# First-layer attention: VectorE in program order, low parts at fixed places, one step for the products with v

## The chip, the cores and the metric

One core of one Trainium2 chip runs the whole kernel. The metric is the device time of one execution in microseconds (us), median of several. In this text PE is the matmul engine (TensorE), DVE is VectorE, ACT is ScalarE, POOL is GpSimd, SP is the engine that issues the loads.

## The reference

Four sandwich-normed layers over x of 1 x 256 x 1024, float32. Each layer does `h = h + rms_norm(mixer(rms_norm(h)))`; the mixer differs by layer. The change touches the first, native sparse attention, with 16 heads of 64 in 4 groups that share keys and values:

```python
q, kc, vc, ks, vs, kw, vw, gl, z = split_cols(u @ w_in, A_SPLITS)
kcmp, vcmp = compress(kc, ...), compress(vc, ...)      # 15 blocks of 32 tokens, gelu MLP
p_c = masked_softmax(q @ kcmp - slopes * dist, dist >= 0);  o_c = p_c @ vcmp
p_s = masked_softmax(q @ ksel - slopes * dist, dist >= 0);  o_s = p_s @ vsel
p_w = masked_softmax(q @ kwin - slopes * dist, mask);       o_w = p_w @ vwin
o = gates[0] * o_c + gates[1] * o_s + gates[2] * o_w   # gates = sigmoid(gl)
return (o * silu(z)) @ w_out
```

At 256 tokens the selected blocks and the window each cover all earlier tokens, so both are plain causal softmaxes with their own keys and values.

## The kernel before, in words

**Products in two parts.** A weight tile of 128 x 1024 is loaded into a `raw` buffer (5 of them), ACT writes its rounded high part `whi`, DVE the rest `wlo` (line 106, "low part" from here on); there are 11 pairs of buffers. A projection then does three matmuls per 128 rows (`mm3`, lines 200 to 202: one *step*). `advance()` (line 68) runs at the end of each weight tile: it gives up the tile's pair of buffers, splits the next tile into parts and issues the next load. A load waits until the low part of the tile five places ahead of it has left its `raw` buffer. Tiles are numbered here by their place in the load list: 26 to 31 are the q projections of groups 1 to 3, 32 to 39 the projections for z, 40 to 47 the weights of the output projection, 48 on the next layer's.

**The stage.** After the compression of the keys and values, the pairs of heads 0 to 7 (`nsa_unit`; pair p belongs to group p // 2) run as a pipeline. The front of a pair is three pieces: `scores_of(0, (0, 1))` (queries 0 to 127, both heads), `scores_of(1, (0,))` and then `finish` (queries 128 to 255, one head each; `finish` also scales all the weights by gate over sum, lines 797 to 807). Each makes one score tile in PSUM per head, `S`, of which there are two buffers; per tile DVE adds the mask and takes the minimum twice (line 294), then ACT the exponentials (line 296). An even pair has `cmp_front` ahead of these (the 15 compressed keys: score, two bias steps, softmax on DVE). The back of a pair is two pieces with transposes (`trans`, line 301) and two with the products with v (`pv`, lines 317, 320; the second adds the compressed branch, line 819); an even pair has `cmp_back` ahead of these.

**Order.** `pipeline` lays the pieces of pair i's front (F) and of pair i-1's back (B) out by the pattern `FFBFBBB` and puts steps of the waiting projections between them from a queue (`fill`, `pop`): two after each piece at first, later one. PE's instructions are issued in exactly the order in which the program is written. On ACT, DVE and POOL the scheduler picks, by readiness in its own model and by priority; low parts and high parts of weights have the priority `LATE = -250`, what the z gate needs `LATEZ = -60`, copies out of PSUM `EARLY = 80`.

**Other places that the change touches.** `keep_q` (line 639) takes a q projection out of PSUM: ACT makes the scaled high part, DVE the low part (line 644). `Gate` multiplies attention output and silu(z) (`silu_tanh`, line 392; line 351) and splits the result into parts for the output projection (lines 359, 360).

Of the kernel before, what the change touches and what calls it, by code (L numbers as in the profile page):

```python
# [10 lines left out]
F32 = mybir.dt.float32  # L11
# [17 lines left out]
POOLED = (6,)  # L29
# [8 lines left out]
def trunk(ctx, tc, I, out):  # L38
# [23 lines left out]
    for n in "bcd":  # L62
        add(n + "_v", *range(8))
        add(n + "_t", *range(20 if n == "c" else 24))
        add(n + "_o", *range(8))
    st = {"load": 0, "split": 0, "next": 0, "held": 0, "parts": 0, "after": [], "most": len(seq)}
    raw, parts = {}, {}

    def advance(most=len(seq)):
        while True:  # L70
            while st["load"] < min(len(seq), st["split"] + NS - st["held"] + max(0, min(3, 8 - st["split"]))):
                i = st["load"]
                if i == X1AT:
                    nc.sync.dma_start(h[:, 1, :], I["x"][1])
                _, k, c = seq[i][0].shape
                if 5 <= i < 8:
                    if i == 5:
                        st["extra"] = big.tile([128, 3, 560], F32, name="oT")
                    t = st["extra"][:, i - 5, :]
                else:  # L80
                    t = wts.tile([128, 1024], F32, name="raw", bufs=NS)[:, :k * c]
                t = t.rearrange("p (k c) -> p k c", k=k)
                dma = nc.sync.dma_start(t, seq[i][0])
                if i == 7:
                    st["dma"] = dma.ins
                raw[i] = t
                st["load"] += 1
            i = st["split"]
            if i >= st["load"] or st["parts"] >= NH or i >= min(most, st["most"]):
                return  # L90
            t = raw.pop(i)
            st["split"] += 1
            if not seq[i][1]:
                parts[i] = t
                st["held"] += 1
                continue
            _, k, c = seq[i][0].shape
            hi, lo = [wts.tile([128, 1024], F32R, name=n, bufs=NH)[:, :k * c].rearrange("p (k c) -> p k c", k=k)
                      for n in ("whi", "wlo")]
            with ExitStack() as after:  # L100
                after.enter_context(tc.high_priority(offset=LATE if i >= 12 else 0))
                for ins in st["after"]:
                    after.enter_context(tc.issue_after(ins))
                ACT.activation(hi, t, AF.Copy)  # L104
                on_pool = i in POOLED
                lo_of = (POOL if on_pool else DVE).tensor_tensor(lo, t, hi.bitcast(F32), op=OP.subtract)  # L106
                if i == max(POOLED):
                    st["pool"] = lo_of.ins
                elif not on_pool:
                    st["lo"] = lo_of.ins  # L110
            parts[i] = (hi, lo)
            st["parts"] += 1

# [101 lines left out]
    def pop():  # L215
        fq.popleft()()
        plan["count"] += 1

    def drain():
        while fq:  # L220
            pop()

    def need(i):

# [3 lines left out]
    def push_proj(use, q=fq, idx=None):  # L228

        t = {}  # L230
        idx = idx or take(2)

        def step(c, k):
            if c == 0 and k == 0:
                t["o"] = ps.tile([128, 2, 256], F32, name="mm", bufs=NMM)
            wh, wl = parts[idx[c]]
            mm3(t["o"][:, c, :], wh[:, k, :], wl[:, k, :], uT[0][:, k, :], uT[1][:, k, :], k == 0, k == 7)
            if k == 7:
                free(idx[c])
                if c == 1:  # L240
                    use(t["o"])
                advance()

        for c in range(2):
            for k in range(8):
                q.append(lambda c=c, k=k: step(c, k))
# [76 lines left out]
    class Gate:  # L323
# [9 lines left out]
                push_proj(lambda z, i=i: self.have_z(i, z))  # L333

        def have_z(self, i, z):
            with tc.high_priority(offset=LATEZ):
                self.w[i] = self.silu(z)
            self.go()

        def have_o(self, p):  # L340
            self.o.add(p)
# [14 lines left out]
        def split(self, i):  # L356
            g, hi, lo = [t[:, 2 * i:2 * i + 2, :] for t in (self.oT, *self.gh)]
            with tc.high_priority(offset=LATEZ):
                ACT.activation(hi, g, AF.Copy)
                DVE.tensor_tensor(lo, g, hi.bitcast(F32), op=OP.subtract)  # L360

        def open(self):

# [25 lines left out]

    tanhs = []  # L390

    def silu_tanh(z):
        w = work.tile([128, 2, 256], F32, name="zw", bufs=2)
        tanhs.append(ACT.activation(w, z, AF.Tanh, scale=0.5))
        DVE.scalar_tensor_tensor(w, w, 1.0, z, op0=OP.add, op1=OP.mult)
        return w

    def out_proj(g, l):
        last = l == 3
# [161 lines left out]
    for hd in range(16):  # L561
        POOL.memset(slc[:, hd // 4, hd % 4:hd % 4 + 1], SLA[4 * (hd // 4) + hd % 2])
    dcmp = const.tile([128, 2, 2, 15], F32, name="dcmp")
    d0 = dcmp[:, 0]
    POOL.iota(d0, pattern=[[-128, 2], [16, 15]], base=31, channel_multiplier=-1,
              allow_small_or_imprecise_dtypes=True)
    POOL.affine_select(out=d0, in_=d0, pattern=[[128, 2], [-16, 15]], base=-31, channel_multiplier=1,
                       fill=NEG, compare_op=OP.is_ge)
    POOL.tensor_scalar(dcmp[:, 1], d0, 0.5, None, op0=OP.mult)
    bm = const.tile([60, 4], F32, name="bm")  # L570
    POOL.memset(bm, 0.5)
    POOL.affine_select(out=bm, in_=bm, pattern=[[-15, 4]], base=0, channel_multiplier=1, fill=0.0,
# [63 lines left out]
    def keep_q(o, g):  # L636


        for j in range(2):
            r, other = HALF[j], HALF[1 - j]  # L640
            hs = slice(4 * g + j, 4 * g + j + 3, 2)
            hi, sc = t["q"][r, hs, :], cq[r, 2 * g:2 * g + 1]
            ACT.activation(hi, o[r], AF.Copy, scale=sc)
            DVE.scalar_tensor_tensor(t["q"][other, hs, :], o[r], sc, hi.bitcast(F32), op0=OP.mult,
                                     op1=OP.subtract)
        ready[g] = plan["count"]

    t = {}
# [65 lines left out]
            f()  # L714
    for g in range(1, 4):
        push_proj(lambda o, g=g: keep_q(o, g))
    for _ in range(9):
        pop()
    hidden_t()
# [4 lines left out]

    ga = Gate(0.5, silu_tanh)
    ga.push()
    CS, PTC = {}, {}

    def cmp_front(g):

# [7 lines left out]
        cs = CS[g] = work.tile([128, 2, 4, 15], F32, name="cs", bufs=2)  # L738
        two = sc[:, 0:256].rearrange("p (a s n) -> p a n s", s=2, n=16)[:, :, 0:15, :]
        DVE.tensor_reduce(out=cs.rearrange("p b a n -> p (b a) n"), in_=two, axis=AX.X, op=OP.add)  # L740
        for b in range(2):
            for c in range(2):
                DVE.tensor_tensor(cs[:, b, 2 * c:2 * c + 2], cs[:, b, 2 * c:2 * c + 2],
                                  dcmp[:, c, b, None, :].to_broadcast([128, 2, 15]), op=OP.add)
        for b in range(2):
            DVE.tensor_tensor(cs[:, b], cs[:, b], slc[:, g, :, None].to_broadcast([128, 4, 15]), op=OP.mult)
        cs8 = cs.rearrange("p b a n -> p (b a) n")
        cm, cl = small(8, "cm", 2), small(8, "cl", 2)
        DVE.tensor_reduce(out=cm, in_=cs8, axis=AX.X, op=OP.max)
        DVE.tensor_scalar(cm, cm, -1e20, None, op0=OP.max)  # L750
        DVE.tensor_tensor(cs8, cs8, cm[:, :, None].to_broadcast([128, 8, 15]), op=OP.subtract)
        ACT.activation(cs, cs, AF.Exp)
        DVE.tensor_reduce(out=cl, in_=cs8, axis=AX.X, op=OP.add)
        DVE.tensor_scalar(cl, cl, 1e-30, None, op0=OP.max)
        DVE.reciprocal(cl, cl)
# [11 lines left out]
    def nsa_unit(p):  # L767
# [25 lines left out]

        def finish():
            scores_of(1, (1,))
            l = t["l"]
            DVE.reciprocal(l, l)
            gv = bass.AP(tensor=gate.tensor, offset=gate.offset + 16 + 2 * p,
                         ap=[list(gate.ap[0]), [1, 2], [16, 2], [48, 2]])
            DVE.tensor_tensor(l.rearrange("p (j r b) -> p j r b", j=2, r=2),  # L800
                              l.rearrange("p (j r b) -> p j r b", j=2, r=2), gv, op=OP.mult)
            for br in range(2):
                for j in range(2):
                    x = (j * 2 + br) * 2
                    P = t["P"][j, br]
                    DVE.tensor_scalar(P[:, 0:128], P[:, 0:128], l[:, x:x + 1], None, op0=OP.mult)  # L806
                    DVE.tensor_scalar(P[:, 128:384], P[:, 128:384], l[:, x + 1:x + 2], None, op0=OP.mult)
# [4 lines left out]
        def pv(br):  # L812
            if br == 0:
                t["o"] = ps.tile([128, 256], F32, name="o", bufs=1)
            o = t["o"]
            pv_pair(o, t["PT", br], v, (br * 256 + g * 64,) * 2, br == 0, False)
            if br == 1:
                for j in range(2):
                    PE.matmul(o[64 * j:64 * j + 64, :], vbd[g][:, 2 * i + j, :], PTC[g], start=False, stop=True)
                evac(ga.oT[:, p, :], o)  # L820
                ga.have_o(p)

        front = [lambda: scores_of(0, (0, 1)), lambda: scores_of(1, (0,)), finish]
        back = [lambda: trans(0), lambda: trans(1), lambda: pv(0), lambda: pv(1)]
        if i == 0:
            front.insert(0, lambda: cmp_front(g))
            back.insert(0, lambda: cmp_back(g))
        return front, back

    trans = out_proj(pipeline([nsa_unit(p) for p in range(8)], ga, "FFBFBBB"), 0)  # L830


    SLB = slopes_of(8)
# [190 lines left out]
        with tc.issue_after(pre.ins):  # L1024
            return ACT.activation(*a, **k)

    def silu_sigmoid(z):
        w = work.tile([128, 2, 256], F32, name="zw", bufs=2)
        after_table(w, z, AF.Sigmoid)
        DVE.tensor_tensor(w, w, z, op=OP.mult)  # L1030
        return w

    v = v_proj(trans)
    kT = big.tile([128, 8, 256], F32, name="kT")
# [123 lines left out]
```

## Time and profile before

| | |
|---|---|
| median of 3 runs | 581.54 us (581.32 to 582.4) |
| the profiled execution, own time | 583.38 us |
| its span, first to last instruction | 581.7 us |
| PE busy | 560.6 us, 96% of the span, granted clock 0.992 on average |
| DVE busy | 420.3 us, 72% |
| ACT busy | 334.5 us, 58% |
| POOL busy | 40.7 us, 7% |
| the loads (queue 1) | 86.09 MB, 43.7% of the 16 DMA engines' time |

The span is the stretch that the trace covers; the execution's own time is 1.7 us longer. The share of busy time is a mean over stages. The chain that ended last is 81% PE, 8% DVE, 4% issue, 2% ACT, 2% DMA. The stage of the change begins some 62 us into the span and ends at 165.19 us, with the first matmul of the output projection.

### The profile page before, as it was taken

The numbers are of one execution on the slowest core, as the hardware profiler recorded it, in microseconds if no ns is written. First come the engines' busy times: TensorE is split into PE (matmuls) and PEld (weight loads), VectorE is DVE, ScalarE is ACT, GpSimd is POOL, SyncE is SP. The second block draws the span as 40 slices with busy tenths as digits, with TensorE's granted clock in tenths as the row PEclk, the third lists the DMA queues.
The fourth block names the chain that finished last, engine by engine and source line by source line (L and its number), as shares of the span: only waits on it lengthen the run. The fifth ranks groups of instructions, "written<-read, shape, count | busy, mean of one in ns | idle before, by whom it ended". The sixth has DMA issues, their size and how long they took to land.

```text
span 581.7 us, 10475 instructions
## 1 busy us (share of the span) xinstructions
PE 560.6 (96%) x3930; PEld 496.8 (85%) x3930; DVE 420.3 (72%) x947; ACT 334.5 (58%) x715; POOL 40.7 (7%) x89
## 2 busy tenths in 40 slices
PE   7999987989999999999999999999999999999995
PEld 6998876777788799999988789999987898888984
DVE  5973898887836896777974886768548778888632
ACT  6752787776824475676642474658524765666410
POOL 1900000000000100000420100000001000000000
PEclk9999998999999999999999999999999999999998
DMA  8774925521250596443352568443525683332002
GB/s 296 247 251 146 319 71 190 168 90 44 74 179 4 180 330 231 147 145 126 120 171 73 181 238 302 149 145 110 177 76 181 233 307 137 120 110 74 1 37 73
DMA packets 27779, 90.96 MB, mean 156 GB/s; under 512 B 4560, under 2 KB 5200, under 8 KB 27728
## 3 DMA queue, kind: packets, MB, share of 16 engines
q1 hardware_dynamic: 26144, 86.09, 43.7%
q10 hardware_dynamic: 1584, 4.20, 2.2%
q8 instruction: 31, 0.51, 0.4%
q14 instruction: 20, 0.16, 0.1%
HBM read 89.22 MB, written 1.05 MB: 155 GB/s over the span
## 4 chain that ended last, share of the span: by engine, by line
PE 81%; DVE 8%; issue 4%; ACT 2%; DMA 2%; POOL 1%; SPq 0%; POOLq 0%; DVEq 0%; ACTq 0%
PE mm L200 16%; PE mm L201 14%; PE mm L202 14%; PE mm L262 6%; PE mm L260 6%; PE mm L261 6%; PE pt L301 3%; DVE wlo L106 3%; PE S L311 3%; PE o L317 2%; ACT whi L104 1%; PE o L655 1%; DVE P L294 1%; DMA h<-in_x_dram 1%; PE pt L188 1%
## 5 line engine op out<-in xcount | busy, mean ns | idle before, releaser
L200 PE MATMUL mm<-uth,whi 128*128 128x256 f32 x736 | 219.0, 298 | 0.0
L106 DVE TENSOR_TENSOR wlo<-raw,whi 128x1024 fp32r<-128x1024 f32 (+1 forms) x153 | 182.3, 1207 | 43.4 <-ACT whi L104 42.8
L201 PE MATMUL mm<-utl,whi 128*128 128x256 f32 x736 | 208.5, 283 | 0.0
L202 PE MATMUL mm<-uth,wlo 128*128 128x256 f32 x736 | 208.3, 283 | 0.0
L104 ACT ACTIVATE whi<-raw 128x1024 fp32r<-128x1024 f32 (+1 forms) x153 | 157.0, 1043 | 73.5 <-PE mm L201 38.5
L200 PEld LDWEIGHTS mm<-uth,whi 128*128 128x128 f32 x736 | 140.9, 191 | 15.5 <-issue 14.7
L201 PEld LDWEIGHTS mm<-utl,whi 128*128 128x128 f32 x736 | 141.1, 192 | 0.9
L202 PEld LDWEIGHTS mm<-uth,wlo 128*128 128x128 f32 x736 | 140.9, 191 | 0.0
L260 PE MATMUL mm<-whi,qT 128*128 128x512 f32 x128 | 50.5, 394 | 0.0
L261 PE MATMUL mm<-whi,kT 128*128 128x512 f32 x128 | 49.9, 390 | 0.0
L262 PE MATMUL mm<-wlo,qT 128*128 128x512 f32 x128 | 49.9, 390 | 0.0
L260 PE MATMUL mm<-whi,uth 128*128 128x512 f32 (+1 forms) x112 | 42.6, 380 | 0.0
L262 PE MATMUL mm<-wlo,uth 128*128 128x512 f32 (+1 forms) x112 | 42.1, 376 | 0.0
L261 PE MATMUL mm<-whi,utl 128*128 128x512 f32 (+1 forms) x112 | 42.1, 376 | 0.0
L294 DVE CUSTOM_DVE_ANT_0 P<-S,mask 128x128 f32<-128x128 f32 (+1 forms) x96 | 30.6, 353 | 8.3 <-PE S L786 6.0
L415 ACT ACTIVATE junk<-mm 128x512 bf16<-128x512 f32 x16 | 9.5, 595 | 42.1 <-PE mm L262 42.1
L296 ACT ACTIVATE P<-P,mxa 128x128 f32<-128x128 f32 (+1 forms) x64 | 28.4, 447 | 3.7 <-DVE mxa L294 3.7
L146 ACT ACTIVATE PT<-pt 128x384 f32<-128x384 f32 x58 | 25.8, 483 | 7.5 <-PE pt L301 7.5
L262 PEld LDWEIGHTS mm<-wlo,qT 128*128 128x128 f32 x128 | 24.0, 188 | 5.0
L260 PEld LDWEIGHTS mm<-whi,qT 128*128 128x128 f32 x128 | 24.1, 188 | 4.7
L261 PEld LDWEIGHTS mm<-whi,kT 128*128 128x128 f32 x128 | 24.1, 188 | 4.7
L301 PE MATMUL pt<-ident,P 128*128 128x128 f32 x180 | 27.0, 279 | 0.5 <-DVE P L806 0.4
(207 smaller groups left out, 757.3 us busy)
## 6 DMA issues: line engine op xcount, KB each, us to landing
raw<-in_a_t_dram SPq DMA_DIRECT2D x24, 512.0 KB, 4.8
raw<-in_b_t_dram SPq DMA_DIRECT2D x24, 512.0 KB, 4.6
raw<-in_d_t_dram SPq DMA_DIRECT2D x24, 512.0 KB, 4.5
raw<-in_c_t_dram SPq DMA_DIRECT2D x20, 512.0 KB, 5.2
raw<-in_w_dram SPq DMA_DIRECT2D x8, 512.0 KB, 4.7
raw<-in_a_o_dram SPq DMA_DIRECT2D x8, 512.0 KB, 3.8
raw<-in_b_v_dram SPq DMA_DIRECT2D x8, 512.0 KB, 3.4
raw<-in_b_o_dram SPq DMA_DIRECT2D x8, 512.0 KB, 3.5
```

The lines of the kernel that those rows point to most:

```text
L104: ACT.activation(hi, t, AF.Copy)
L106: lo_of = (POOL if on_pool else DVE).tensor_tensor(lo, t, hi.bitcast(F32), op=OP.subtract)
L146: ACT.activation(dst, src, AF.Copy)
L200: PE.matmul(o, sh, mh, start=first, stop=False)
L201: PE.matmul(o, sh, ml, start=False, stop=False)
L202: PE.matmul(o, sl, mh, start=False, stop=last)
L260: PE.matmul(o, sh, wh[:, j, c0:c1], start=k == 0, stop=False)
L261: PE.matmul(o, sl, wh[:, j, c0:c1], start=False, stop=False)
L262: PE.matmul(o, sh, wl[:, j, c0:c1], start=False, stop=k == 7)
L294: DVE.tensor_tensor_reduce(out=P[:, c0:c1], in0=S, in1=mask[:, c0:c1], scale=-slope, scalar=BIG, op0=OP.add, op1=OP.min, accum_out=mx)
L296: ACT.activation(P[:, c0:c1], P[:, c0:c1], AF.Exp, bias=mx, scale=-1.0, accum_out=l)
L301: PE.transpose(pt[:, i, :], P[:, i * 128:(i + 1) * 128], ident)
```

## The change

Within the stage, DVE's instructions too are now issued in the order of the program (`manual_schedule` from the 15 steps ahead of `cmp_front(0)` to the end of the pipeline). Low parts of weights that are split within the stage are kept back and written at set places: one in `first` (unless the second half of the compressed softmax stands there), one in `second`, one in `finish` ahead of the scaling, and in any case when the tile or the one before it begins; what is left comes at the stage's end. What DVE does with a result of ACT (low part of q, silu, low part of the gated output) is written three steps later (`later(3, ...)`); the second half of the compressed softmax comes after the first scores of the pair. Six small additions and multiplications per group become two. Both products with v of a pair are one piece, and the pattern is `FFBFBB`. In the other layers the same functions run at once.

```diff
+    def low_parts(n):
+        for i in sorted(low)[:n]:
+            low.pop(i)()
+    def later(n, f):
+        if st["own"]:
+            waiting.append((plan["count"] + n, f))
+        else:
+            f()
+    def overdue(everything=False):
+        while waiting and (everything or waiting[0][0] <= plan["count"]):
+            waiting.popleft()[1]()
...
                 ACT.activation(hi, t, AF.Copy)
-                on_pool = i in POOLED
-                lo_of = (POOL if on_pool else DVE).tensor_tensor(lo, t, hi.bitcast(F32), op=OP.subtract)
...
+                low[i] = lambda i=i, t=t, hi=hi, lo=lo: low_part(i, t, hi, lo)
+                if not st["own"]:
+                    low.pop(i)()
...
     def pop():
         fq.popleft()()
         plan["count"] += 1
+        overdue()
...
+            for i, at in ((idx[c], 0), (idx[c] + 1, 2)):
+                if k == at and i in low:
+                    low.pop(i)()
             wh, wl = parts[idx[c]]
             mm3(t["o"][:, c, :], wh[:, k, :], wl[:, k, :], uT[0][:, k, :], uT[1][:, k, :], k == 0, k == 7)
...
+    own = ExitStack()
+    own.enter_context(tc.manual_schedule(engines={mybir.EngineType.DVE}))
+    st["own"] = True
     for _ in range(9):
         pop()
     hidden_t()
...
-        for b in range(2):
-            for c in range(2):
-                DVE.tensor_tensor(cs[:, b, 2 * c:2 * c + 2], cs[:, b, 2 * c:2 * c + 2],
-                                  dcmp[:, c, b, None, :].to_broadcast([128, 2, 15]), op=OP.add)
-        for b in range(2):
-            DVE.tensor_tensor(cs[:, b], cs[:, b], slc[:, g, :, None].to_broadcast([128, 4, 15]), op=OP.mult)
+        pairs = cs.rearrange("p b (c j) n -> p (b c) j n", j=2)
+        DVE.tensor_tensor(pairs, pairs, dcmp.rearrange("p b c n -> p (b c) n")[:, :, None, :]
+                          .to_broadcast([128, 4, 2, 15]), op=OP.add)
+        DVE.tensor_tensor(cs, cs, slc[:, g, None, :, None].to_broadcast([128, 2, 4, 15]), op=OP.mult)
...
         ACT.activation(cs, cs, AF.Exp)
+        CHALF.append(lambda: cmp_weights(g, cs, cs8, cl))
...
         def finish():
             scores_of(1, (1,))
+            low_parts(1)
             l = t["l"]
             DVE.reciprocal(l, l)
...
+        def pvs():
+            pv(0)
+            pv(1)
...
+        def first():
+            scores_of(0, (0, 1))
+            if CHALF:
+                CHALF.pop()()
+            else:
+                low_parts(1)
+        def second():
+            scores_of(1, (0,))
+            low_parts(1)
-        front = [lambda: scores_of(0, (0, 1)), lambda: scores_of(1, (0,)), finish]
-        back = [lambda: trans(0), lambda: trans(1), lambda: pv(0), lambda: pv(1)]
+        front = [first, second, finish]
+        back = [lambda: trans(0), lambda: trans(1), pvs]
...
-    trans = out_proj(pipeline([nsa_unit(p) for p in range(8)], ga, "FFBFBBB"), 0)
+    gh = pipeline([nsa_unit(p) for p in range(8)], ga, "FFBFBB")
+    low_parts(len(seq))
+    st["own"] = False
+    own.close()
+    trans = out_proj(gh, 0)
```

The low parts of `keep_q`, of silu and of the gated output are wrapped in `later(3, ...)` in the same way.

## Rows read from the trace of the kernel before

**Rows 1.** Part 1 of the page: engine, busy us (share of the span), instructions.
```profile
PE 560.6 (96%) x3930; PEld 496.8 (85%) x3930; DVE 420.3 (72%) x947; ACT 334.5 (58%) x715; POOL 40.7 (7%) x89
```

**Rows 2.** Windows: stretch, length, busy PE, PEld, DVE, ACT, POOL; clock, DMA share, GB/s.
```profile
62.00:102.00 40.00, 33.52 (x258) 30.26 (x258) 36.93 (x120) 32.38 (x77) 0.00 (x0) 0.96 0.53 184
102.00:162.00 60.00, 57.66 (x440) 45.56 (x441) 49.27 (x207) 43.57 (x135) 1.16 (x4) 1.00 0.31 98
```

**Rows 3.** Timeline of PE, 79 to 98 us: start, length, engine, line, [idle <-releaser].
```profile
79.31 0.40 PE L785 MATMUL S<-kT,qT 128*128 128x512 f32 x1
...
92.43 0.39 PE L785 MATMUL S<-kT,qT 128*128 128x256 f32 x1 [1.12 <-DVE cs L740]
...
97.79 0.77 PE L785 MATMUL S<-kT,qT 128*128 128x512 f32 x1 [2.78 <-DVE cm L750]
```

**Rows 4.** Windows of PE alone around 98 us: stretch, length, busy, clock, DMA, GB/s.
```profile
98.00:98.60 0.60, 0.60 (x2) 0.50 0.77 314
...
100.40:101.00 0.60, 0.60 (x7) 0.68 0.00 0
```

**Rows 5.** Timeline of DVE, 69 to 87 us.
```profile
69.83 1.40 DVE L701 TENSOR_TENSOR v<-o,bm 60x256 f32<-60x256 f32 x4
...
77.71 0.42 DVE L294 CUSTOM_DVE_ANT_0 P<-S,mask 128x256 f32<-128x256 f32 x1
...
79.34 1.18 DVE L106 TENSOR_TENSOR wlo<-raw,whi 128x1024 fp32r<-128x1024 f32 x1
...
83.03 3.50 DVE L106 TENSOR_TENSOR wlo<-raw,whi 128x1024 fp32r<-128x1024 f32 x3
```

**Rows 6.** Timeline of SP, the loads from 84 us.
```profile
84.74 2.24 SPq L83 DMA_DIRECT2D raw<-in_a_t_dram  x3
```

**Rows 7.** Timeline of ACT, the high part that waits for such a load.
```profile
89.10 1.06 ACT L104 ACTIVATE whi<-raw 128x1024 fp32r<-128x1024 f32 x1 [1.59 <-DMA raw<-in_a_t_dram]
```

**Rows 8.** Timeline of DVE, end of pair 4, its scaling, and that of pair 7.
```profile
126.49 0.42 DVE L294 CUSTOM_DVE_ANT_0 P<-S,mask 128x256 f32<-128x256 f32 x1 [1.61 <-PE S L786]
...
127.18 0.29 DVE L294 CUSTOM_DVE_ANT_0 P<-S,mask 128x128 f32<-128x128 f32 x1
...
127.39 0.29 DVE L294 CUSTOM_DVE_ANT_0 P<-S,mask 128x128 f32<-128x128 f32 x1
...
130.32 0.28 DVE L806 TENSOR_SCALAR P<-P,la 128x128 f32<-128x128 f32 x1
...
132.16 0.42 DVE L294 CUSTOM_DVE_ANT_0 P<-S,mask 128x256 f32<-128x256 f32 x1
...
154.22 0.20 DVE L797 RECIPROCAL la<-la 128x8 f32<-128x8 f32 x1
...
154.65 0.29 DVE L806 TENSOR_SCALAR P<-P,la 128x128 f32<-128x128 f32 x1
```

**Rows 9.** Timeline of PE, scores of pair 5.
```profile
127.41 0.36 PE L785 MATMUL S<-kT,qT 128*128 128x256 f32 x1 [0.37 <-DVE mxa L294]
...
128.08 0.40 PE L785 MATMUL S<-kT,qT 128*128 128x512 f32 x1
```

**Rows 10.** Groups by line and form, 62 to 162 us: busy, mean ns | idle before.
```profile
L644 DVE SCALAR_TENSOR_TENSOR qT<-mm,cq,qT 64x512 fp32r<-64x512 f32 x8 | 6.0, 750 | 0.7 <-ACT qT L643 0.5
...
L743 DVE TENSOR_TENSOR cs<-cs,dcmp 128x30 f32<-128x30 f32 x16 | 1.9, 185 | 0.0
```

**Rows 11.** Timeline of PE around the two products with v of one pair.
```profile
112.75 0.28 PE L201 MATMUL mm<-utl,whi 128*128 128x256 f32 x1
112.86 0.28 PE L202 MATMUL mm<-uth,wlo 128*128 128x256 f32 x1
...
113.56 0.39 PE L320 MATMUL o<-PT,v 128*64 128x128 f32 x4
113.87 0.39 PE L200 MATMUL mm<-uth,whi 128*128 128x256 f32 x1
...
114.42 0.65 PE L317 MATMUL o<-PT,v 128*64 128x256 f32 x4
```

More of the change, by code (lines that the diff above doesn't have):

```diff
@@ L65, in trunk, with low_part @@
         add(n + "_o", *range(8))
-    st = {"load": 0, "split": 0, "next": 0, "held": 0, "parts": 0, "after": [], "most": len(seq)}
-    raw, parts = {}, {}
+    st = {"load": 0, "split": 0, "next": 0, "held": 0, "parts": 0, "after": [], "most": len(seq), "own": False}
+    raw, parts, low = {}, {}, {}
+    waiting = deque()
+    def low_part(i, t, hi, lo):
+        on_pool = i in POOLED
+        lo_of = (POOL if on_pool else DVE).tensor_tensor(lo, t, hi.bitcast(F32), op=OP.subtract)
+        if i == max(POOLED):
+            st["pool"] = lo_of.ins
+        elif not on_pool:
+            st["lo"] = lo_of.ins
+    def low_parts(n):
[9 more added lines that the diff above has]
+            waiting.popleft()[1]()
     def advance(most=len(seq)):
@@ L104, in advance @@
                 ACT.activation(hi, t, AF.Copy)
-                on_pool = i in POOLED
-                lo_of = (POOL if on_pool else DVE).tensor_tensor(lo, t, hi.bitcast(F32), op=OP.subtract)
[L107 to L110, printed above, removed]
+                low[i] = lambda i=i, t=t, hi=hi, lo=lo: low_part(i, t, hi, lo)
+                if not st["own"]:
+                    low.pop(i)()
             parts[i] = (hi, lo)
@@ L221, in drain @@
             pop()
+        overdue(True)
     def need(i):
@@ L335, in have_z, with got @@
         def have_z(self, i, z):
+            def got(w):
+                self.w[i] = w
+                self.go()
             with tc.high_priority(offset=LATEZ):
-                self.w[i] = self.silu(z)
-            self.go()
+                self.silu(z, got)
         def have_o(self, p):
@@ L359, in split @@
                 ACT.activation(hi, g, AF.Copy)
-                DVE.tensor_tensor(lo, g, hi.bitcast(F32), op=OP.subtract)
+                later(3, lambda: DVE.tensor_tensor(lo, g, hi.bitcast(F32), op=OP.subtract))
         def open(self):
@@ L390, in trunk, with silu_tanh, rest @@
     tanhs = []
-    def silu_tanh(z):
+    def silu_tanh(z, got):
         w = work.tile([128, 2, 256], F32, name="zw", bufs=2)
         tanhs.append(ACT.activation(w, z, AF.Tanh, scale=0.5))
-        DVE.scalar_tensor_tensor(w, w, 1.0, z, op0=OP.add, op1=OP.mult)
-        return w
+        def rest():
+            DVE.scalar_tensor_tensor(w, w, 1.0, z, op0=OP.add, op1=OP.mult)
+            got(w)
+        later(3, rest)
     def out_proj(g, l):
@@ L563, in trunk @@
     dcmp = const.tile([128, 2, 2, 15], F32, name="dcmp")
-    d0 = dcmp[:, 0]
+    d0 = dcmp[:, :, 0]
     POOL.iota(d0, pattern=[[-128, 2], [16, 15]], base=31, channel_multiplier=-1,
@@ L568, in trunk @@
                        fill=NEG, compare_op=OP.is_ge)
-    POOL.tensor_scalar(dcmp[:, 1], d0, 0.5, None, op0=OP.mult)
+    POOL.tensor_scalar(dcmp[:, :, 1], d0, 0.5, None, op0=OP.mult)
     bm = const.tile([60, 4], F32, name="bm")
@@ L643, in keep_q @@
             ACT.activation(hi, o[r], AF.Copy, scale=sc)
-            DVE.scalar_tensor_tensor(t["q"][other, hs, :], o[r], sc, hi.bitcast(F32), op0=OP.mult,
-                                     op1=OP.subtract)
+            later(3, lambda r=r, other=other, hs=hs, hi=hi, sc=sc: DVE.scalar_tensor_tensor(
+                t["q"][other, hs, :], o[r], sc, hi.bitcast(F32), op0=OP.mult, op1=OP.subtract))
         ready[g] = plan["count"]
@@ L726, in trunk @@
     ga.push()
-    CS, PTC = {}, {}
+    CS, PTC, CHALF = {}, {}, []
     def cmp_front(g):
@@ L752, in cmp_front, with cmp_weights @@
         ACT.activation(cs, cs, AF.Exp)
+        CHALF.append(lambda: cmp_weights(g, cs, cs8, cl))
+    def cmp_weights(g, cs, cs8, cl):
         DVE.tensor_reduce(out=cl, in_=cs8, axis=AX.X, op=OP.add)
@@ L816, in pv @@
             pv_pair(o, t["PT", br], v, (br * 256 + g * 64,) * 2, br == 0, False)
[L817 to L821, printed above, removed]
-        front = [lambda: scores_of(0, (0, 1)), lambda: scores_of(1, (0,)), finish]
-        back = [lambda: trans(0), lambda: trans(1), lambda: pv(0), lambda: pv(1)]
+        def pvs():
+            pv(0)
+            pv(1)
+            o = t["o"]
+            for j in range(2):
+                PE.matmul(o[64 * j:64 * j + 64, :], vbd[g][:, 2 * i + j, :], PTC[g], start=False, stop=True)
+            evac(ga.oT[:, p, :], o)
+            ga.have_o(p)
+        def first():
[9 more added lines that the diff above has]
+        back = [lambda: trans(0), lambda: trans(1), pvs]
         if i == 0:
@@ L1025, in after_table, with silu_sigmoid @@
             return ACT.activation(*a, **k)
-    def silu_sigmoid(z):
+    def silu_sigmoid(z, got):
         w = work.tile([128, 2, 256], F32, name="zw", bufs=2)
@@ L1030, in silu_sigmoid @@
         DVE.tensor_tensor(w, w, z, op=OP.mult)
-        return w
+        got(w)
     v = v_proj(trans)
```

## The prediction

> **What bounds the kernel now.** I read the page first: PE is busy 96% of the span, so time is gained only where PE stands still, runs at the lower clock, or has less to do [rows 1]. Next, windows over the stage that is changed. It falls in two. From 62 to 102 us PE worked 33.52 of 40 us while DVE worked 36.93: DVE is the bound there, and PE lost 6.48 us. From 102 to 162 us PE worked 57.66 of 60 and DVE 49.27: PE is the bound and lost only 2.34 us [rows 2]. So all that better order on DVE can give back is 6.48 + 2.34 = 8.8 us, and what the clock cost. Then the timeline, for who is waited for: PE's score matmuls wait for DVE, 1.12 us at 92.43 and 2.78 us at 97.79 [rows 3]. Both are the same wait: there are two `S` buffers, and a third score tile cannot begin until DVE has taken its two minima of the first. After the second wait the granted clock is 0.50 (1.2 GHz) and comes back about 100.8 [rows 4]; 3.0 us at half speed cost about 1.45 us.
>
> **The change, part by part.** I wrote out both programs' order for the stage, piece by piece, with the queue's counts; the steps and pieces below are from there.
>
> *Products with v in one piece.* Before, the last matmuls of the first product start at 113.56, one step lies between, and the second product starts at 114.42: 0.86 us. Without the step the next thing starts 0.31 us later (113.56 to 113.87). The step that is moved costs three matmuls at a pitch of 0.11 to 0.12, 0.36 us, elsewhere [rows 11]. Saved: 0.86 - 0.31 - 0.36 = 0.19 us a pair, 1.5 us for eight pairs, all on PE. The step between hid ACT's copies of the second pair of transposes; if that cover fails, the 0.19 is lost again, so -1.5 to 0. I take **-1.5**.
>
> *The scaling now stands ahead of the next pair's minima.* This is the largest part. After an even pair's `finish` come, with one step between each (two for pair 2), the odd pair's `first` and `second`. `second`'s score tile needs the buffer that the minima of `first` free. Before, DVE took these minima as soon as the scores were there (127.18) and did low part and scaling later [rows 8]. Now the program's order holds: two minima of pair 4 (126.49 to 127.18, 0.69), a low part (a third of 3.50, 1.17, [rows 5]), reciprocal and gate until the scaling starts (154.22 to 154.65, 0.43), eight scalings (130.32 to 132.16, 1.84), two minima of pair 5 (2 x 0.21 from 127.18 to 127.39, 0.42) [rows 8]. That is 4.55 us one after another, from 126.49 to 131.04. PE had issued this score tile at 128.08 [rows 9]: it comes 3.0 us later, and nothing lies on PE to fill the time, since its order is fixed and everything behind this matmul waits too. Pair 6 to 7 has the same order: 3.0. Between pairs 2 and 3 the two low parts of q stand there as well (2 x 0.750, [rows 10]) and PE has one more step to do: 3.0 + 1.5 - 0.36 = 4.1. Together +10.1. What goes: the later half's idle time, 2.34 less the 0.37 that pairs 5 and 7 each have inside the figure above [rows 9], 1.6. So **+8.5** (7 to 10: below, if ACT or PE is late anyway; above, if DVE also waits for the exponentials ahead of the reciprocal).
>
> *Low parts at fixed places, early stretch.* Before, DVE finishes the four copies `v` at 71.2 and does no low part until 79.34; by then it has the last minima of pair 0 behind it (77.71 + 0.42 = 78.1) [rows 5], so that the `second` scores of pair 1 start at 79.31 [rows 3]. Now the low part of tile 37 must come ahead of those last minima of pair 0, and that of 38 and the scaling of pair 0 ahead of pair 1's first. Tile 37 is not there yet: its load waits for the buffer of tile 32, hence for the low parts of 31 and 32, which the scheduler still places itself. From such a load's issue (84.74, [rows 6]) to the end of its high part (89.10 + 1.06, [rows 7]) is 5.4 us. Either the low parts of 31 to 36 fill DVE's gaps ahead of it, or DVE stands and takes them then. Upper end: eight low parts (31 to 38) x 1.17 = 9.4, with 0.43 + 1.84 + 0.42 for scaling and minima, less 0.5 for the merged small instructions (next part): 78.1 + 11.6 = 89.7 against 79.31, +10.4. Lower end: five low parts (31 to 33, 37, 38), +6.9. I take the middle, +8.6. DVE has then done work that it did later before, so the waits of 1.12 and 2.78 and the 1.45 of the clock go: -5.35. Net **+3.2** (1.5 to 5.0).
>
> *Clock.* PE now stands for about 3 us or more four times (at the end of the early stretch, and at pairs 3, 5 and 7). The one such wait of before, 2.78 us, was followed by the lower clock at a cost of 1.45 [rows 3, 4]. Between nothing and 4 x 1.45 = 5.8 I take 0.85 each, **+3.4**, since the clock may be up again before the wait ends. The Trainium skill ("TensorE: Matmul & The Clock Gate", section "Part 1: The HAM clock gate") says that an idle PE is put to the lower clock and gets the higher one back only by sustained work. Rows 3 and 4 agree for their one case; by the rule all four would pay in full, and the sum would be 2.4 higher.
>
> *Merged small instructions.* Sixteen additions of 185 ns become four, eight multiplications four [rows 10]; four instructions fewer a group, up to 0.74 us of DVE less what the larger ones take longer: 0 to 0.74. I count 0.5 in group 0 (above) and nothing for groups 1 to 3, where PE has transposes and steps to do meanwhile. The Trainium skill ("Perfetto Trace Analysis", section "Optimizing Scalar/DVE Operations") holds that grouping into larger operations pays where the engine is saturated. By rows 2 that is the early stretch; by the rule group 1 would count too, and the sum would be 0.5 lower.
>
> *The rest, at 0.* Low parts of q, silu and gated output three steps later: they replace waits of DVE for ACT, and PE needs them a whole tile later; if that cover is gone one instruction of 0.75 [rows 10] is in the way each time. Low parts of 48 to 50 at the stage's end hold back three loads; the output projection hides them, and uncovered they cost one such load, 5.4 us. In layers 2 to 4 the gating runs at a lower priority than before, at most one low part (1.17) either way in each.
>
> **Sum.** -1.5 + 8.5 + 3.2 + 3.4 = +13.6 us. The profiled execution took 583.38 us in all (span 581.7 and 1.7 around it), so 597.0 for such a one. The median of the runs shown is 581.54, 1.8 below it: **595.1 us**.
>
> **Rivals.**
> (a) *Milder*: few low parts get ahead early (+1.5 net), the clock holds: 1.5 + 8.5 - 1.5 = +8.5, 590.0 us. For it: 1.12 us of waiting left no trace on the clock. Against: the new waits are longer than the 2.78 that did.
> (b) *Worse*: upper ends everywhere, 5.0 + 10 + 5.8 - 1.5 = +19.3, 600.8 us. For it: ACT's high part of 1.06 us may stand ahead of an exponential that DVE's fixed order now waits for.
> (c) *Faster*: the low parts fall into gaps ahead of 71 us and DVE no longer lets the small instructions of the compressed softmax come between two minima, so the `S` buffers come free in time. Place: the early stretch; price: all of its loss, 6.48 + 1.45 = 7.9; with 1.6 and 1.5 from above that is -11.0 against +10.1, 580.6 us. It decides as soon as pair 1's `second` scores start no later than 79.3 and the scaling costs the next pair no more than it gives back. Against it: 36.93 of 40 us leaves DVE no gap for six low parts [rows 2].
> (d) *Nothing*: the scheduler's order was in effect the program's. Against: it took the minima ahead of the scaling at 127.18 [rows 8]. 581.5 us.
>
> **How the numbers follow.** Forecast 0.42 (its own range 591 to 599), (a) 0.24, (b) 0.17, (c) 0.13, (d) 0.04. The range runs from a little below (a) to the top of (b), 584 to 603; outside lie (c), (d) and the far end of (b). About 0.2% (1.2 us) can be told from no change by a measurement of this kernel: faster 0.13, same 0.04, slower 0.83.
>
> **What would show it.** In the profile after: the `second` score tile of pairs 3, 5 and 7 preceded by 3 to 4 us of idle PE that a minimum of DVE ends, with eight scalings and a low part just ahead of that minimum; three or four stretches at a clock of 0.5; the stage's end, 165.19 before, about 13 to 14 us later, and everything behind it shifted by that. The products with v would follow each other 0.31 us after the last matmuls of the first. I am wrong if PE's idle time from 62 us to the output projection is no more than 8.8 us, or if these score tiles do not wait.

## The result and the profile after

The changed kernel took **603.38 us** (602.38 to 603.81, 4 runs) against 581.97 us for the kernel before (581.32 to 585.17, 4 runs): a ratio of 1.0354, interval 1.0313 to 1.0395. It is slower, as forecast, but by 21.4 us and not by 13.6. The profiled execution took 602.38 us, its span is 600.7 us: 19.0 more than the one before, at a mean granted clock of 0.974 (0.992 before).

Part 1 of the page of the changed kernel; it answers to [rows 1]:
```profile
PE 564.7 (94%) x3930; PEld 502.5 (84%) x3930; DVE 422.0 (70%) x931; ACT 335.0 (56%) x715; POOL 41.4 (7%) x89
```
The work is the same, PE just stands still longer. Where, the windows say (columns as in [rows 2]); the second one here runs to the stage's end, which is later than before:
```profile
62.00:102.00 40.00, 28.53 (x193) 25.34 (x193) 33.09 (x92) 26.29 (x57) 0.00 (x0) 0.79 0.57 203
102.00:185.00 83.00, 70.47 (x524) 60.05 (x525) 53.78 (x217) 51.55 (x153) 1.16 (x4) 0.92 0.17 53
```
In the early stretch PE now loses 11.47 us (6.48 before), and DVE, which bounded it, is busy *less*: 33.09 of 40 us against 36.93. So it isn't that DVE has more to do; it does it in another order, with waits of its own. Windows of PE alone over the whole stage, up to the first matmul of the output projection, first of the kernel before, then of the changed one (stretch, length, busy, clock, DMA, GB/s). On PE's timeline this matmul starts at 165.03 before; the 165.19 above is the chain's time for it:
```profile
62.00:165.03 103.03, 94.21 (x721) 0.98 0.39 129
```
```profile
62.00:184.00 122.00, 97.99 (x712) 0.87 0.30 103
```
The stage ends 18.97 us later: 15.19 us of it is idle time (24.01 against 8.82), the other 3.78 are PE's busy time, whose matmuls last longer at the lower clock. The timeline of PE in the changed kernel names the waits, which answer to [rows 3, 9]:
```profile
77.62 0.76 PE L823 MATMUL S<-kT,qT 128*128 128x512 f32 x1 [5.59 <-DVE mxa L321]
...
83.91 0.36 PE L823 MATMUL S<-kT,qT 128*128 128x256 f32 x1 [2.20 <-DVE mxa L321]
...
85.73 0.55 PE L823 MATMUL S<-kT,qT 128*128 128x256 f32 x1 [1.35 <-DVE mxa L321]
...
89.56 0.77 PE L823 MATMUL S<-kT,qT 128*128 128x512 f32 x1 [1.78 <-DVE mxa L321]
...
118.45 0.77 PE L823 MATMUL S<-kT,qT 128*128 128x512 f32 x1 [5.03 <-DVE mxa L321]
...
144.35 0.47 PE L823 MATMUL S<-kT,qT 128*128 128x512 f32 x1 [3.01 <-DVE mxa L321]
...
166.21 0.71 PE L823 MATMUL S<-kT,qT 128*128 128x512 f32 x1 [3.01 <-DVE mxa L321]
```
All are score matmuls that wait for minima (`mxa`) of DVE. The summary of PE's waits puts it in one row (total, times, longest):
```profile
PE S L823 <- DVE mxa L321: 23.2, 10, 5.6
```
What stood ahead of the minima is in the timeline of DVE. In the early stretch:
```profile
70.47 1.21 DVE L72 TENSOR_TENSOR wlo<-raw,whi 128x1024 fp32r<-128x1024 f32 x1
71.60 0.27 DVE L779 TENSOR_TENSOR cs<-cs,dcmp 128x120 f32<-128x120 f32 x1
71.79 1.21 DVE L72 TENSOR_TENSOR wlo<-raw,whi 128x1024 fp32r<-128x1024 f32 x1
...
75.65 1.21 DVE L72 TENSOR_TENSOR wlo<-raw,whi 128x1024 fp32r<-128x1024 f32 x1
...
76.98 0.27 DVE L321 CUSTOM_DVE_ANT_0 P<-S,mask 128x128 f32<-128x128 f32 x1
...
79.17 0.28 DVE L791 TENSOR_REDUCE cl<-cs 128x8 f32<-128x120 f32 x1 [1.28 <-ACT cs L787]
```
Five low parts of 1.21 us stand between the small dependent instructions of the compressed scores, which follow each other within 0.2 to 0.3 us where nothing stands between them. They are written ahead of the region with the fixed order, so they still go where the scheduler puts them; experiment 5, which holds them back, moves them out of these gaps. At pairs 3 and 5:
```profile
113.86 0.20 DVE L836 RECIPROCAL la<-la 128x8 f32<-128x8 f32 x1 [0.63 <-ACT P L323]
...
116.25 1.51 DVE L678 SCALAR_TENSOR_TENSOR qT<-mm,cq,qT 64x512 fp32r<-64x512 f32 x2
117.79 0.29 DVE L321 CUSTOM_DVE_ANT_0 P<-S,mask 128x128 f32<-128x128 f32 x1
...
140.29 1.22 DVE L72 TENSOR_TENSOR wlo<-raw,whi 128x1024 fp32r<-128x1024 f32 x1
...
141.87 0.29 DVE L845 TENSOR_SCALAR P<-P,la 128x128 f32<-128x128 f32 x1
...
143.44 0.35 DVE L846 TENSOR_SCALAR P<-P,la 128x256 f32<-128x256 f32 x1
143.70 0.29 DVE L321 CUSTOM_DVE_ANT_0 P<-S,mask 128x128 f32<-128x128 f32 x1
```
Low part, reciprocal, gate and eight scalings, at pair 3 also the two low parts of q (1.51), and only then the minima: the order that the prediction wrote out. Behind these waits PE runs at its lower clock (windows of PE, as [rows 4]):
```profile
84.00:90.00 6.00, 2.86 (x11) 0.53 0.50 166
90.00:96.00 6.00, 6.00 (x32) 0.62 0.30 100
...
116.00:120.00 4.00, 1.55 (x5) 0.50 0.04 12
120.00:124.00 4.00, 4.00 (x28) 0.76 0.41 131
...
146.00:150.00 4.00, 4.00 (x22) 0.60 0.00 0
...
166.00:170.00 4.00, 3.79 (x15) 0.57 0.04 15
```

### The profile page after: what moved, and what is told of

Same layout as the page of the kernel before. It is cut to its first block, busy times and chain, and to the rows that moved or that the text cites. A ratio compares the mean times of both kernels' runs of the same rounds, so it can differ in the third digit from the quotient of the medians.

```text
span 600.7 us, 10456 instructions
## 1 busy us (share of the span) xinstructions
PE 564.7 (94%) x3930; PEld 502.5 (84%) x3930; DVE 422.0 (70%) x931; ACT 335.0 (56%) x715; POOL 41.4 (7%) x89
## 4 chain that ended last, share of the span: by engine, by line
PE 79%; DVE 9%; issue 5%; ACT 2%; DMA 2%; POOL 1%; SPq 0%; POOLq 0%; DVEq 0%; ACTq 0%
PE mm L222 15%; PE mm L223 14%; PE mm L224 14%; PE mm L289 6%; PE mm L287 6%; PE mm L288 6%; DVE wlo L72 3%; PE pt L328 3%; PE S L338 3%; PE o L344 2%; ACT whi L129 1%; PE o L689 1%; PE S L823 1%; PE pt L210 1%; DMA h<-in_x_dram 1%
## 5 line engine op out<-in xcount | busy, mean ns | idle before, releaser
L222 PEld LDWEIGHTS mm<-uth,whi 128*128 128x128 f32 x736 | 143.1, 194 | 14.6 <-issue 13.3
L223 PEld LDWEIGHTS mm<-utl,whi 128*128 128x128 f32 x736 | 143.0, 194 | 1.2
L224 PEld LDWEIGHTS mm<-uth,wlo 128*128 128x128 f32 x736 | 142.5, 194 | 0.0
L321 DVE CUSTOM_DVE_ANT_0 P<-S,mask 128x128 f32<-128x128 f32 (+1 forms) x96 | 29.1, 353 | 18.1 <-PE S L824 15.8
L823 PE MATMUL S<-kT,qT 128*128 128x256 f32 (+1 forms) x32 | 13.9, 440 | 23.3 <-DVE mxa L321 23.2
L823 PEld LDWEIGHTS S<-kT,qT 128*128 128x128 f32 x32 | 7.0, 217 | 25.5 <-issue 24.4
```

The costliest lines, as they stand in the source:

```text
L222: PE.matmul(o, sh, mh, start=first, stop=False)
L223: PE.matmul(o, sh, ml, start=False, stop=False)
L224: PE.matmul(o, sl, mh, start=False, stop=last)
L321: DVE.tensor_tensor_reduce(out=P[:, c0:c1], in0=S, in1=mask[:, c0:c1], scale=-slope, scalar=BIG, op0=OP.add, op1=OP.min, accum_out=mx)
L823: PE.matmul(s, q, KH[:, g, :, 0:n], start=True, stop=False)
```

## The experiments

The theory: VectorE is needed by PE at a few moments only, and the fixed order puts the even pair's scaling (8.5 us) and early low parts ahead of the minima that PE wants; the lower clock adds its price to each wait. The rivals: the cost comes from the fixed order as such, from the one-piece products, or from the waits being handed on whatever the order.

**1. The scaling behind the odd pair's first minima.** The changed kernel, with
```diff
+            if i == 0: SCALE.append(scale)
+            else: scale()
+        def scale():
...
         def first():
             scores_of(0, (0, 1))
+            if SCALE: SCALE.pop()()
```


> The changed kernel with one thing moved: reciprocal, gate and eight scalings of an even pair stand behind the odd pair's first minima and no longer ahead of them. Theory 1 (the scaling ahead of the next pair's minima holds the score buffers): at pairs 3, 5 and 7 the idle time of PE ahead of the second scores falls from 5.0, 3.0 and 3.0 us to below 3, 1 and 1 us (2.3 us less each), the clock stays up at pairs 5 and 7, and the time falls by 8 to 12 us, to 591 to 595. Rival (it is the low part in finish, or the fixed order as such, that holds the buffers): the waits fall by less than 1 us each and the time stays above 600.

Measured: 594.67 us, ratio to before 1.0201 (1.0167 to 1.0235), 8.7 us less than the changed kernel. Its timeline of PE:
```profile
113.77 0.60 PE L823 MATMUL S<-kT,qT 128*128 128x512 f32 x1 [2.04 <-DVE mxa L321]
...
137.57 0.47 PE L823 MATMUL S<-kT,qT 128*128 128x512 f32 x1 [0.73 <-DVE mxa L321]
...
148.89 0.58 PE L823 MATMUL S<-kT,qT 128*128 128x256 f32 x1 [2.11 <-DVE cs L777]
```
The waits of pairs 3 and 5 fell from 5.03 to 2.04 and from 3.01 to 0.73 (pair 7 as pair 5), with a granted clock of 1.00 behind the short ones. A new one stands at pair 6: the S buffer of group 3's compressed scores is freed by a sum that is now late itself. Pair 1's wait of 1.78 went too, since pair 0's scaling is moved as well. So the scaling's place is 8.7 us for all four even pairs, net of what came in its stead.

**2. Without the fixed order.** The changed kernel without the line `own.enter_context(tc.manual_schedule(...))`; low parts are still kept back and written at their places.

> The changed kernel with all its moved pieces, but DVE's order is left to the scheduler again (the low parts that were kept back are still written at their places and so have the priority of that place). Theory 1 (the fixed order is the cause of the whole loss): near the kernel before less the 1.5 us of the one-piece products, 579 to 583 us. Rival (the places at which low parts and delayed instructions are written cost on their own): 585 to 600, with the waits at pairs 3, 5 and 7 still above 2 us.

Measured: 591.12 us, ratio 1.0149 (1.0117 to 1.018). The time is in the rival's range, the waits are not all as it had them: those of pairs 5 and 7 went, 4.32 us at pair 3 stayed, and its DVE timeline, and then PE's, show a new one:
```profile
90.65 4.62 DVE L72 TENSOR_TENSOR wlo<-raw,whi 128x1024 fp32r<-128x1024 f32 x4
95.19 0.28 DVE L844 TENSOR_SCALAR P<-P,la 128x128 f32<-128x128 f32 x1
...
97.14 0.41 DVE L776 TENSOR_REDUCE cs<-S 128x120 f32<-128x240 f32 x1
```
```profile
97.60 0.58 PE L822 MATMUL S<-kT,qT 128*128 128x256 f32 x1 [8.35 <-DVE cs L776]
```
Low parts that are kept back and written late take the priority of where they are written; four go in a row, ahead of pair 1's scaling and of the sum that frees PE's buffer. Leaving the order to the scheduler gives back some 12 of the 21 us; how much of the rest is the keeping back, experiment 8 asks.

**3. The products in one piece alone.** The kernel before, with `pv(0)` and `pv(1)` as one piece and the pattern `FFBFBB`.

> The kernel before with the two products with v in one piece and the pattern FFBFBB, nothing else. Theory: 0.19 us a pair on PE, 1.5 us less in all, 580.0 to 581.0 against 582. Rival (the step between the products hides ACT's copies of the second transposes, or the other spread of the steps costs): no change or up to 2 us more.

Measured: 583.7 us against 583.56, ratio 1.0009 (0.9985 to 1.0032): no change. PE's busy time fell from 560.6 to 558.3 us, but the time is there again as idle time: from 62 to 165 us 11.23 us against 8.82, most of the growth behind 102 us (4.55 against 2.34). In its timeline the first of these waits was 2.78 in [rows 3], the second is new:
```profile
97.50 0.47 PE L785 MATMUL S<-kT,qT 128*128 128x512 f32 x1 [2.82 <-DVE mxa L294]
...
107.73 0.36 PE L785 MATMUL S<-kT,qT 128*128 128x256 f32 x1 [1.52 <-DVE mxa L294]
```

**4. The clock held up.** The changed kernel, with seven matmuls that nobody reads where PE would wait (ahead of `second`'s scores at pairs 3, 5, 7; the trace has each as two instructions, 3.19 us of work at each place):
```diff
+            if i == 1 and p > 1:
+                warm = ps.tile([128, 256], F32, name="o", bufs=1)
+                for _ in range(7):
+                    PE.matmul(warm, ident, mov, start=True, stop=True)
```


> The changed kernel with seven matmuls more, whose result nobody reads, ahead of the second scores of pairs 3, 5 and 7, where PE would stand idle for 3 to 5 us. They fill time that PE waits anyway. Theory (the lower clock after these waits costs 1.3 to 1.7 us each): the granted clock stays at 1.0 at pairs 5 and 7 at least, and the time falls by 2 to 4 us, to 599 to 601.5. Rival (behind the wait PE is not the bound for the next microseconds, so the lower clock is hidden): the clock stays up and the time is the same within 1 us. If the added matmuls last longer than the wait, it rises.

Measured: 599.28 us, ratio 1.0275 (1.0244 to 1.0307): 4.1 us less than the changed kernel by the medians, 4.6 by the ratios, the minima coming no earlier. Its windows of PE:
```profile
116.00:120.00 4.00, 2.38 (x17) 1.00 0.00 0
120.00:124.00 4.00, 3.98 (x32) 1.00 0.52 159
...
146.00:150.00 4.00, 4.00 (x38) 1.00 0.02 4
```
From 146 to 150 us PE does 38 matmuls at a clock of 1.00, where the changed kernel does 22 at 0.60. Its profiled execution (597.36 us) is 5.0 us faster than the changed kernel's, and 0.82 of that was gained before the first of these matmuls; the other 4.2, like the 4.1 to 4.6 of the medians, put the lower clock at 1.4 to 1.5 us for each of these three waits. The other three executions, at a mean clock of 0.979 against 0.988 in this one, took 1.9 to 2.5 us longer; where their clock was lower no trace shows.

**5 and 6. Low parts held back earlier, alone and with edit 1.** The low parts of tiles 31 and up wait for their places from the compress loop on, and pair 0 and pair 1's `first` take none:
```diff
-                if not st["own"]:
+                if i < st["keep"]:      # 31; the number of tiles after the stage
                     low.pop(i)()
...
-            low_parts(1)
+            low_parts(p > 0)
```


> After, with the low parts of weight tiles 31 and up kept back from the compress loop on (not only from the start of the fixed order), and none taken in pair 0 and at pair 1's first place; what a projection step needs is still done where it falls due. Theory (the early stretch is late because eight low parts of 1.2 us stand in front of pair 0's and pair 1's minima): the five that sit in the gaps of the compressed scores' chain and three behind them go, 8 x 1.2 = 9.7 us of VectorE, so pair 1's second scores start near 80.5 instead of 89.6, the half clock behind them is less, and the time falls by 5 to 9 us, to 594 to 598, the low parts being paid in VectorE's idle time of pairs 2 to 7. Rival (the gaps between the dependent small instructions would have stood idle anyway, so the low parts in them were nearly free): pair 1's second scores come 2 to 4 us earlier at most, and the low parts added to pairs 2 to 7 cost as much again: 601 to 606.

> The edit of e5_hold_early together with that of e1_scaling_later (the even pair's scaling behind the odd pair's first minima). Theory (the two causes stand at different places and add): 603.4 - 8.7 - (5 to 9) = 585.5 to 590, still above the kernel before, since the low parts now stand among pairs 2 to 7. Rival (with the scaling out of the way the low parts taken at pairs 4 to 7 become the next wait of TensorE there): 591 to 596, with waits on VectorE of over 1.5 us at pairs 5 and 7.

Measured: 599.77 us (ratio 1.0287, 1.0259 to 1.0315) alone, 3.6 us less than the changed kernel, between both expectations; 587.72 us (1.0069, 1.0046 to 1.0093) together with edit 1, 15.7 less, as the theory said. Alone, from PE's timeline:
```profile
83.05 0.77 PE L823 MATMUL S<-kT,qT 128*128 128x512 f32 x1 [2.72 <-DVE mxa L321]
...
149.48 0.58 PE L823 MATMUL S<-kT,qT 128*128 128x256 f32 x1 [1.63 <-DVE cs L777]
```
Pair 1's second scores came at 83.05 instead of 89.56 (7.6 earlier, as this trace's stage begins 1.1 us later), and by the stage's end (181.19) 3.7 us of that was lost again, 1.63 of it in the new wait at 149.48. Low parts now stand between the minima of the last pairs, where the changed kernel has none; that they make this wait is argued, not tested. Together with edit 1 the waits at pairs 5 and 7 are 0.73, so the rival's next wait wasn't there but at the group's sum (first row PE, then DVE ahead of it):
```profile
140.38 0.58 PE L823 MATMUL S<-kT,qT 128*128 128x256 f32 x1 [2.85 <-DVE cs L777]
```
```profile
136.43 0.29 DVE L851 TENSOR_SCALAR P<-P,la 128x128 f32<-128x128 f32 x1
...
139.93 0.40 DVE L777 TENSOR_REDUCE cs<-S 128x120 f32<-128x240 f32 x1
```
Kernel 6 keeps the fixed order and is 3.4 us faster than kernel 2 without it. So most of the cost lay not in fixing the order as such, but in what this order puts first. What the last 0.7% over the kernel before are I did not separate.

**7. The merged small instructions alone**, in the kernel before.

> Before, with the compressed scores' six small instructions per group merged into two and nothing else. Theory (VectorE stands on the path in the early stretch alone, where group 0's chain gets some 0.5 us shorter): 0 to -0.6 us, a ratio of 0.999 to 1.000. Rival (the scheduler puts a low part in the place that comes free, as it did in the changed kernel's early stretch): 0 to +1.5 us.

Measured: 582.49 us, ratio 0.9974 (0.9956 to 0.9992): faster by 0.5 to 2.6 us, a little more than expected. The profiled span is 581.7 us as before, so the trace doesn't show where.

**8. Free order, low parts written where the weights arrive.** The kernel of 2, with `low.pop(i)()` at once.

> The kernel of e2_free_order (after without the fixed order on VectorE), with the low parts written out where the weights arrive again, as before the change; what waits for ScalarE is still put three steps later. Theory (in the free order the 8 us that were left came from the low parts that were kept back and then ran four in a row ahead of pair 1's scaling): the waits of 8.35 us at the compressed scores of group 1 and of 4.3 us behind it go, 581 to 585. Rival (putting three steps later what waits for ScalarE, or the compressed weights' own place, costs by itself): 587 to 592, with a wait of over 3 us left at the same place.

Measured: 586.3 us, ratio 1.005 (1.0031 to 1.007), between both. The 8.35 us became 4.31, of the size that the merged kernel of 7 has there (4.03); 4.33 us at pair 3 stayed. So keeping low parts back cost 4.8 of what 2 had left. What the last 3.8 us over 7 are (work put three steps later, the compressed weights' place, the products) I did not separate.

**9 to 11. Moving the next wait away.** 9 is 6 with the odd pairs' scaling deferred too (`if p < 7: SCALE.append(scale)`). 10 and 11 are 7, with `tc.high_priority(offset=EARLY)` around the compressed scores' first sum (10) or their whole chain (11).

> The kernel of e6_both with the odd pairs' scaling moved behind the next pair's first minima as well (the last pair's stays). Theory (the second scores of pairs 2, 4 and 6 wait for the group's first sum, which stands behind the odd pair's reciprocal and eight scalings, 2.2 us of the wait of 2.85 us at 140.38): that wait falls under 1 us, the half clock behind it goes, and the time falls by 2 to 5 us, to 583 to 586. Rival (the odd pair's transposes follow close behind the next first scores and then wait for the scaling themselves): 586.5 to 590, with waits of over 1 us of the transposes on VectorE.

> The kernel of e7_merge_only with a higher priority for one instruction a group, the first sum over the compressed scores, so that in the free order it goes ahead of the pair's scaling and of the low parts. Theory (the wait of 4.03 us at group 1's second scores is only a matter of the place of that sum in VectorE's order, as the waits of the changed kernel are): the wait falls under 1.5 us and the half clock behind it goes: 577 to 580, faster than both kernels. Rival (the wait is handed on to the transposes, which want the scaling that is now later by as much, or the scheduler moves other work into the place): 581 to 585.

> The kernel of e7_merge_only with the higher priority for the whole chain of small instructions over the compressed scores, not for its first sum alone. Theory (in e10_reduce_early the wait of 2.98 us before pair 2's later scores came from the rest of the chain and the low part of 1.22 us in its middle, which stood between the scaling and pair 2's minima): with the chain in among the scalings these minima come 1.5 to 2.5 us earlier, the wait falls under 1.5 us and the granted clock stays at 1.00: 577.5 to 580.5 us. Rival (the low part and q's low parts fall before the minima all the same, so the wait only changes its place): 581 to 583.

Measured: 592.34 us (1.0145, 1.0116 to 1.0175), 4.6 *slower* than 6; 581.9 us (0.9967, 0.9952 to 0.9982); 583.41 us (0.9996, 0.9977 to 1.0015). The rivals' mechanisms held in all three, 9 coming out 2.3 us above its rival's range and 11 by 0.4. PE's timelines, one row each:
```profile
123.87 1.16 PE L328 MATMUL pt<-ident,P 128*128 128x128 f32 x6 [2.80 <-DVE P L851]
```
```profile
97.44 0.47 PE L784 MATMUL S<-kT,qT 128*128 128x512 f32 x1 [2.98 <-DVE cm L749]
```
```profile
96.94 0.47 PE L784 MATMUL S<-kT,qT 128*128 128x512 f32 x1 [3.67 <-DVE mxa L294]
```
In 9 the transposes wait for the scaling instead; in 10 and 11 the wait of 4.03 us leaves one matmul and stands before the next. From 88 to 97 us DVE is busy for 8.26 of the 9 us in 10 and for 7.62 in 11, where it waits itself (0.42 for PE, 0.64 for ACT). So these two orders only chose who waits. Kernels 7 and 10 beat both kernels, by 0.3% as timed; neither's profiled span (581.7, 581.5) differs from before's, so I call it a small gain from fewer instructions and no more.

## Why the prediction was right, and where it was too low

The direction, the mechanism and the places at pairs 3, 5 and 7 were right; in the early stretch the loss came as four waits from pair 0 on, not as one at its end. The size was 8.3 us short: 595.1 against 603.38, which is 0.4 past the top of the range, 603 (as ratios to the kernel before, each by its own median, 1.0354 lies within 603 / 581.54 = 1.0369). Of this, 2.8 us are the profiled executions' places among their runs: I took 1.8 off for before, and the changed kernel's is 1.0 below its median. The other 5.4 are terms:

| term | predicted | measured |
|---|---|---|
| early stretch, PE idle | 8.6 - 1.12 - 2.78 = +4.7 | 11.47 - 6.48 = +5.0 |
| scaling ahead of the minima, PE idle | +8.5 | 12.54 - 2.34 = +10.2 |
| clock, net of the 1.45 before | +1.95 | about +7.1 |
| products in one piece, PE busy | -1.5 | -2.3 (experiment 3) |
| sum | +13.6 | +20.0 |

The last column's sum belongs to a stage that begins about 1.0 us earlier in the changed trace, so 19.0 on the stage's end and on the span. The clock's figure is an estimate, what is left: PE's busy time in the stage grew by 3.78, with 2.3 saved on the products and 1.0 us less work in the window from 62 us.

**Scaling.** Pairs 5 and 7 waited 3.01 us each, predicted 3.0. Pair 3 waited 5.03, predicted 4.1: its reciprocal waited another 0.63 us for ScalarE's exponential, the case that I had put at the upper end. And of the small waits that I let go (1.6), three stayed: 0.44 at 134.03, 0.37 at 140.52 and 0.37 at 162.38. Experiment 1 shows the cause.

**Early stretch.** Pair 1's second scores came 10.25 us later on the trace's clock, 11.3 from the stage's start, against 6.9 to 10.4. I had asked how many low parts get ahead: all eight did, five of them in the gaps of a dependent chain. That the waits of [rows 3] at 92 and 98 us then go held: no wait of DVE on PE's timeline between 89.56 and 118.45.

**Clock: the step that failed in size.** I took 0.85 us for each of four waits, below the one price that I had (1.45), because the clock might be up again early. It was not. Experiment 4 puts three of them at 4.1 to 4.6 us together. By difference (7.1 + 1.45 - 4.3) the early stretch lost some 4.2, since there it isn't one wait but four in a row, and the granted clock is 0.61 on average from 74 to 96 us. The two rows from 84 to 96 us alone give 1.3 and 2.3 by an estimate, busy time times what the clock lacked. So the term of +3.4 for the clock was mis-sized: it measured some 8.5. The Trainium skill ("TensorE: Matmul & The Clock Gate", section "Part 1: The HAM clock gate") holds that an idle PE drops to the lower clock and has to earn the higher one back by sustained work. The traces agree for the waits of 3.01 and 5.03 us, with 0.50 to 0.60 behind them, and the sum by it, 2.4 higher, was the better one.

**Products.** The cover didn't fail: after the last matmuls of the first product the next begins 0.22 us later:
```profile
126.90 0.39 PE L347 MATMUL o<-PT,v 128*64 128x128 f32 x4
127.12 0.60 PE L344 MATMUL o<-PT,v 128*64 128x256 f32 x4
```
But experiment 3 shows that the saving is worth nothing where the next matmul waits for DVE anyway. I had counted it in full because PE is the bound from 102 us on; there PE's busy time fell, and its idle time grew by as much (2.34 to 4.55 us). So DVE is a close second there. What the saving is worth in the changed kernel no run shows.

**Merged instructions.** Half a microsecond inside the early stretch was not to be seen, since the gaps that the chain left were filled with low parts. Alone, experiment 7, they gave 1.5 us (0.5 to 2.6). The Trainium skill ("Perfetto Trace Analysis", section "Optimizing Scalar/DVE Operations") holds that grouping can pay on a saturated engine. The 0.3% agrees; that it came from the stretch where DVE is saturated, no trace here shows.

**Rivals.** (b), 600.8 us with all upper ends and the wait for an exponential, was the nearest. (c) fell at its own condition: pair 1's second scores were not there by 79.3.

## What to carry to other kernels

An order written by hand for an engine that isn't the bound must be read from the side of the engine that is: list which of its instructions the other waits for, and let nothing that can wait (a scaling for a later transpose, a low part for a later tile) stand ahead of them; experiment 9 shows the limit, where the transposes came so soon that they waited instead. Where two buffers alternate, one late minimum stops the whole fixed order behind it, and each stop of about 3 us costs half as much again in clock. And where the engine has hardly a gap left, as here from 88 to 97 us, two other orders only handed the wait on; fewer instructions gave 0.3%.

## What the runs showed of the hardware that was not expected

The price of a wait doesn't go by its length alone. In the kernel of experiment 6 a wait of 2.18 us, at 78.82, left the granted clock at 1.00, one of 2.04 us, at 104.97, brought it down to 0.63 in the stretch behind (PE's timeline, then its windows):
```profile
78.82 0.36 PE L823 MATMUL S<-kT,qT 128*128 128x256 f32 x1 [2.18 <-DVE mxa L321]
...
104.97 0.47 PE L823 MATMUL S<-kT,qT 128*128 128x512 f32 x1 [2.04 <-DVE mxa L321]
```
```profile
76.00:80.00 4.00, 1.60 (x12) 1.00 0.00 0
...
82.00:86.00 4.00, 4.00 (x35) 1.00 0.06 12
...
102.00:106.00 4.00, 1.96 (x13) 0.95 0.38 132
106.00:110.00 4.00, 4.00 (x23) 0.63 0.15 24
```
PE even had less work in the row with the first wait (1.60 us) than in the row with the second (1.96), so what tells the two apart stays open. And seven matmuls with no reader at each of three waits, which bring nothing forward themselves, gained 4.1 us: work on PE can be cheaper than none.
